# First stage of a Hymba layer: x loaded channel-major instead of token-major and transposed

## The chip, the core and the metric

One NeuronCore of a Trainium2 chip runs the whole layer in one launch. The metric is the time of one execution on the device, in microseconds (us). The engines are named as the profile names them: PE is the matrix engine (TensorE), PEld its weight loads, DVE the VectorE, ACT the ScalarE, POOL the GpSimd, SP the engine that only issues transfers. Each engine works through its own queue of instructions in order and waits on semaphores of the others; a waiting instruction holds up everything behind it on the same engine.

## What is computed

The layer takes x (1024 tokens by 1024 channels, float32) and a vector cond, from which shifts, scales and gates are made. The change touches the beginning of the first of three sublayers:

```python
def rms_norm(x, gain):
    y = xf * lax.rsqrt(jnp.mean(xf * xf, axis=-1, keepdims=True) + EPS)
    return (y * gain.astype(jnp.float32)).astype(x.dtype)

def modulate(h, shift, scale):
    return h * (1 + scale[:, None, :]) + shift[:, None, :]

def swiglu(h, w_gate, w_up, w_down):
    return (jax.nn.silu(h @ w_gate) * (h @ w_up)) @ w_down
...
    c_act = jax.nn.silu(cond)
    mod = c_act @ w_mod[l] + b_mod[l]
...
    h = modulate(rms_norm(x, ffn1_norm[l]), sh1, sc1)
    x = x + 0.5 * g1[:, None, :] * swiglu(h, ffn1_w_gate[l], ffn1_w_up[l], ffn1_w_down[l])
```

The mean of squares runs over the 1024 channels of a token. What is called x after this stage is the modulated h; the original x is loaded again much later for the residual.

## The kernel before

The products need h with channels on the 128 partitions and tokens along the free axis. There are 8 channel tiles (k = 0 to 7) and two halves of 512 tokens (h = 0, 1), so 16 tiles `x[k][h]` of 128x512. To keep float32 accuracy each operand is split in two parts of a shorter float32 format: ACT casts it to the part `hi`, DVE subtracts to get `lo`, and a product is three matmuls (`mm3`, line 330: hi·hi, hi·lo, lo·hi). For activations the split is `shifted` and `lows`, for weights it is `weight` (a cast and a subtraction of 128x1024).

The stage around the change builds four products (`part`, line 926; outputs 0 and 2 are gate columns, 1 and 3 the up columns that go with them) over 8 k-tiles and two halves: 64 parts of three matmuls, 192 matmuls in all, named `p` in the profile. When they are done PE goes on with the next group of the same sublayer, named `fa1`.

Before a `p` matmul can run on a tile, this is done:

- x is loaded token-major (`tok_load`, from a second copy of x): eight tiles `xb` of 128 tokens by 1024 channels, four for each half. With tokens on partitions the sum of squares is one instruction with an accumulator for each tile (`squares`, line 848), on DVE or ACT by choice.
- `root_of` turns the four sums of a half into four columns of 1/rms: a small DVE instruction and a power on POOL.
- `scaled` multiplies the tokens' rows by it, in pieces of some k-tiles: on ACT, a small piece on POOL.
- `turned` (line 892) transposes: four PE transposes of 128x128 for each k and h, into a PSUM tile `pt`; 16 such groups in all.
- `shifted` (line 898) on ACT reads `pt`, applies the channel's scale and shift, writes `x[k][h]`, and casts it to `hi`; `lows` on DVE makes `lo`.
- `mods_of(k)` (line 858) makes the scale and the shift of the 128 channels of k: two DVE reductions over a loaded tile `mw` of 1 MB.

`kept_busy` puts matmuls whose result nobody reads on PE (named `filler`).

The order of everything in the stage is the order of the source (`InOrder.strict` ties each engine's instructions to their order in the code); there is no planner here. Lines 935 to 1018 are that order. All loads are issued from SP in the order of the code: four tiles of x, one `mw`, two raw weight tiles, the other four tiles of x, and so on.

Of the kernel before, what the change touches and what calls it, by code (L numbers as in the profile page):

```python
# [40 lines left out]
ENDS = 2, 3, 6, 7  # L41
J = S // TAU
# [189 lines left out]
def hymba_layer(ctx: ExitStack, tc, x_d, xt_d, wm1_d, wmod_d, gu1_d, gs1_d, ds10_d, ds11_d, wl1_d, win_d, wcvb_d, wout_d, glu_d, gu2_d, gs2_d, wd2_d, ds20_d, ds21_d, ds22_d, wl2_d, cols_d, cond_d, lam_d, bc_d, out_d):  # L232
# [575 lines left out]
    tok_open = ExitStack()  # L808
    tok = tok_open.enter_context(tc.tile_pool(name="tok", bufs=1, side="right"))
# [7 lines left out]
    mw, xb = [], []  # L817
    pre = t2k("pre")[:, :KT]
    st = t2k("st")
    junks = [mov(f"junk{i}", dtype=F32)[:].rearrange("p a b -> p (a b)") for i in range(2)]  # L820

    def mod_load(n=1):
        for _ in range(n):
            k = len(mw)
            mw.append(pro.tile([P, 2, 1024], F32, tag="mw", name=f"mw{k}", bufs=3))
            SP.dma_start(mw[k][:], wm1_d[k])

    def tok_load(n):
        for _ in range(n):
            b = len(xb)  # L830
            if b < 4:
                xb.append(tok.tile([P, D], F32, tag=f"xb{b}", name=f"xb{b}")[:])
            else:
                xb.append(mov(f"xb{b}", dtype=F32)[:].rearrange("p a b -> p (a b)"))
            SP.dma_start(xb[b], xt_d[b])

    tok_load(4)
    mod_load()
    ws.load(2)

# [7 lines left out]
    def squares(b, engine):  # L848

        if engine is A:  # L850
            A.activation(junks[-1], xb[b], AF.Square, accum_out=st[:, b : b + 1])
        else:
            other = junks[0]
            V.tensor_tensor_reduce(
                out=other, in0=xb[b], in1=xb[b], scale=1.0, scalar=0.0, op0=ALU.mult, op1=ALU.add, accum_out=st[:, b : b + 1]
            )
# [11 lines left out]
    root = [None, None]  # L868
# [5 lines left out]
    def scaled(h, lo, hi, engine=A):  # L874

        for b in range(4):
            part, by = xb[4 * h + b][:, lo * P : hi * P], root[h][:, b : b + 1]
            if engine is A:
                A.activation(part, part, AF.Identity, scale=by)
            else:  # L880
                engine.tensor_scalar(out=part, in0=part, scalar1=by, scalar2=None, op0=ALU.mult)

    turns = {}
    filler = ps("filler")

    def kept_busy(n, lhsT, rhs):

        for _ in range(n):
            T.matmul(filler[:], lhsT=lhsT, rhs=rhs, start=True, stop=True)


    def turned(h, k):

        turns[h, k] = sm([P, HALF], f"pt{k}_{h}")
        for b in range(4):
            T.transpose(turns[h, k][:, b * P : (b + 1) * P], xb[4 * h + b][:, k * P : (k + 1) * P], ident[:])

    def shifted(h, k):

        hi, lo = act1[h][k] = parts(f"h1{k}_{h}")  # L900
        A.activation(x[k][h], turns.pop((h, k))[:], AF.Identity, bias=mods[:, 0, k : k + 1], scale=scl[:, 0, k : k + 1])
        A.copy(hi, x[k][h])

    def lows(h, k):
        hi, lo = act1[h][k]
        V.tensor_tensor(out=lo, in0=x[k][h], in1=hi.bitcast(F32), op=ALU.subtract)

    w4 = []

    def weight(home):  # L910
        ws.open(home, 1)
        w4.extend(ws.take())
# [22 lines left out]
    squares(0, V)  # L935
    squares(1, V)
    silu(0)
    silu(1)
    squares(2, A)
    squares(3, V)  # L940
    tok_load(4)
    mod_load()
    ws.load(4)
    mod_load()
    kept_busy(4, ident[:], xb[0][:, :HALF])
    root_of(0)
    scaled(0, 0, 2)
    mods_of(0)
    mod_load()
    turned(0, 0)  # L950
# [3 lines left out]
    turned(0, 1)  # L954
    part(0, 0, (0,))
    weight(ringp)
    part(0, 0, (1,))
    kept_busy(18, w4[0][:, 0, :P], act1[0][0][0])
    squares(4, A)
    squares(5, A)  # L960
    squares(6, V)
    squares(7, V)
    scaled(0, 2, 8)
    root_of(1)
    scaled(1, 0, 2)
    scaled(1, 2, 4, nc.gpsimd)
    turned(1, 0)
    kept_busy(3, w4[0][:, 0, :P], act1[0][0][0])
    mods_of(1)
    mod_load()  # L970
    weight(ringp)
    shifted(1, 0)
    shifted(0, 1)
    lows(1, 0)
    mods_of(2, (0,))
    turned(1, 1)
    part(1, 0, (0, 1, 2))
    part(0, 0, (2,))
    lows(0, 1)
    turned(0, 2)  # L980
    shifted(1, 1)
    part(0, 1, (0, 1, 2))
    lows(1, 1)
    mods_of(2, (1,))
    mod_load()
    turned(1, 2)
    shifted(0, 2)
    part(1, 1, (0, 1, 2))
    lows(0, 2)
    mods_of(3)  # L990
    mod_load()
    shifted(1, 2)
    scaled(1, 4, 8)
    lows(1, 2)
    for k in range(2, KT):
        if k + 1 < KT:
            turned(0, k + 1)
        part(0, k, (0, 1, 2))
        if k + 1 < KT:
            turned(1, k + 1)  # L1000
            shifted(0, k + 1)
            shifted(1, k + 1)
        if k + 2 < KT:
            mods_of(k + 2)
            if k + 5 < KT:
                mod_load()
        if k + 1 < KT:
            lows(0, k + 1)
            lows(1, k + 1)
        if k == 5:  # L1010
            weight(ringp)
        part(1, k, (0, 1, 2))
    for h in range(2):
        part(h, 0, (3,))
    gu_first(0)
    for k in range(1, KT):
        for h in range(2):
            part(h, k, (3,))
    InOrder.strict = False
    tok_open.close()  # L1020
# [3 lines left out]
    ws.free(3)  # L1024
    ws.free()
# [958 lines left out]
_ORDER = ["x", "xt", "wm1", "wmod", "gu1", "gs1", "ds10", "ds11", "wl1", "win", "wcvb", "wout", "glu", "gu2", "gs2", "wd2", "ds20", "ds21", "ds22", "wl2", "cols", "cond", "lam", "bc"]  # L1984
# [17 lines left out]
```

## Time and profile before

| | |
|---|---|
| median of 3 runs | 1650.75 us (1650.39 to 1652.87) |
| profiled execution | 1650.02 us, of it the span that the profile shows 1648.3 us |
| PE busy | 1631.4 us (99%) |
| DVE busy | 1142.9 us (69%) |
| ACT busy | 721.8 us (44%) |
| POOL busy | 177.7 us (11%) |

The span begins with the first instruction and all times in rows are counted from there. PE's share of busy time counts pipelined matmuls and is no measure of its speed, but a stretch without a gap on PE means that PE is what the stretch waits for. The stage of the change reaches from the start of the span to 75.44 us, where the first `fa1` matmul starts.

### The profile page before, as it was taken

To read this page: it belongs to the slowest core of one execution; us is meant where nothing else is said; L and a number is where in the kernel's file an instruction comes from. 1 tells how busy PE (TensorE), PEld (TensorE's weight loads), DVE (VectorE), ACT (ScalarE), POOL (GpSimd) and SP (SyncE) were. 2 spreads that over 40 slices of the span, in tenths; PEclk is the share of its full clock that TensorE was granted. 3 is DMA by queue.
4 is the path that set the end of the run, shared out by engine and by line. 5 is a ranking of instruction groups with operands and counts; after the bars stand their busy time and mean duration, and the time that the engine had idled before them with its cause. 6 is when DMAs were issued, how large, how long until landed. Compare 5 with 4: busy or idle time off the path is not lost.

```text
span 1648.3 us, 20569 instructions
## 1 busy us (share of the span) xinstructions
PE 1631.4 (99%) x7437; PEld 1347.6 (82%) x7437; DVE 1142.9 (69%) x1688; ACT 721.8 (44%) x1072; POOL 177.7 (11%) x219
## 2 busy tenths in 40 slices
PE   8999999999999999999999999999999999999997
PEld 5888888888888888888888888888888888888887
DVE  7984487878576758887887898755565655344576
ACT  6654333333454442463234546344444444322345
POOL 2010000000100102200000030000101100010004
PEclk9999999999999999999999999999999999999999
DMA  9466789898987775668774534477788787889732
GB/s 359 141 161 159 216 221 279 248 265 245 284 242 199 199 225 199 211 199 232 202 196 142 183 102 151 118 205 216 210 221 222 216 221 217 298 250 352 225 71 102
DMA packets 130871, 346.34 MB, mean 210 GB/s; under 512 B 16849, under 2 KB 40657, under 8 KB 129746
## 3 DMA queue, kind: packets, MB, share of 16 engines
q1 hardware_dynamic: 112338, 278.97, 48.6%
q0 software_dynamic: 18432, 66.07, 23.1%
q8 instruction: 58, 0.95, 0.2%
q14 instruction: 43, 0.35, 0.1%
HBM read 261.75 MB, written 74.84 MB: 204 GB/s over the span
## 4 chain that ended last, share of the span: by engine, by line
PE 92%; DVE 3%; ACT 1%; issue 1%; DMA 1%; POOL 1%; SPq 0%; POOLq 0%; DVEq 0%; ACTq 0%
PE wo L113 5%; PE fbd_1B L113 3%; PE fbd_0B L113 3%; PE u L113 3%; PE fad_0B L113 3%; PE fad_1B L113 3%; PE p L113 3%; PE fald L113 2%; PE fbd_1C L113 1%; PE fbd_0C L113 1%; PE gl L113 1%; PE fb0d L113 1%; PE fad_1C L113 1%; PE fad_0C L113 1%; PE fb10d L113 1%; PE fb0u L113 1%
## 5 line engine op out<-in xcount | busy, mean ns | idle before, releaser
L113 DVE TENSOR_TENSOR w<-raw,w 128x1024 fp32r<-128x1024 f32 (+1 forms) x256 | 309.4, 1209 | 235.3 <-ACT w L113 234.8
L113 ACT CAST w<-raw 128x1024 fp32r<-128x1024 f32 (+1 forms) x256 | 266.2, 1040 | 287.6 <-DMA raw<-in_ds 59.9
L175 POOL DMA_DIRECT2D raw<-in_gs x80 | 70.4, 883 | 732.4 <-DVE w L113 431.1
L113 DVE CUSTOM_DVE_ANT_0 wm<-wm,cact 128x1024 f32<-128x1024 f32 x56 | 74.4, 1347 | 2.9 <-DMA wm<-in_wmod 2.9
L175 POOL DMA_DIRECT2D raw<-in_ds x36 | 31.5, 877 | 310.2 <-DVE w L113 207.4
L113 PE MATMUL p<-h,w 128*128 128x512 f32 x192 | 49.0, 404 | 2.0 <-ACT h L113 1.5
L113 PE MATMUL wo<-oa,w 128*128 128x512 f32 x192 | 45.1, 392 | 0.0
L113 PE MATMUL wo<-ob,w 128*128 128x512 f32 x192 | 44.9, 392 | 0.0
L113 PE MATMUL u<-h,w 128*128 128x512 f32 x192 | 44.4, 391 | 0.0
L113 PEld LDWEIGHTS p<-h,w 128*128 128x128 f32 x192 | 35.3, 190 | 10.4 <-ACT h L113 2.0
L113 PEld LDWEIGHTS u<-h,w 128*128 128x128 f32 x192 | 35.8, 188 | 7.6 <-issue 0.3
L113 PEld LDWEIGHTS wo<-ob,w 128*128 128x128 f32 x192 | 35.7, 188 | 7.4
L113 PEld LDWEIGHTS wo<-oa,w 128*128 128x128 f32 x192 | 35.7, 188 | 7.2
L175 POOL DMA_DIRECT2D raw<-in_wcvb x12 | 10.6, 880 | 145.9 <-DVE w L113 69.1
L113 PE MATMUL fb0u<-h,w 128*128 128x512 f32 x96 | 23.8, 391 | 0.0
L113 PE MATMUL fb0g<-h,w 128*128 128x512 f32 x96 | 23.2, 389 | 0.0
L113 PE MATMUL fald<-fa9lA,w 128*128 128x512 f32 x96 | 22.8, 392 | 0.0
L113 PE MATMUL gl<-yg,w 128*128 128x512 f32 x96 | 22.7, 392 | 0.0
L113 PE MATMUL fald<-fa0lA,w 128*128 128x512 f32 x96 | 22.4, 389 | 0.0
L113 PE MATMUL fald<-fa10lA,w 128*128 128x512 f32 x96 | 22.4, 389 | 0.0
L113 PEld LDWEIGHTS fb0g<-h,w 128*128 128x128 f32 x96 | 18.0, 188 | 3.8
L113 PEld LDWEIGHTS fald<-fa0lA,w 128*128 128x128 f32 x96 | 18.0, 188 | 3.7
(1656 smaller groups left out, 4039.1 us busy)
## 6 DMA issues: line engine op xcount, KB each, us to landing
raw<-in_gs SPq DMA_DIRECT2D x80, 512.0 KB, 4.7
raw<-in_gs POOLq DMA_DIRECT2D x80, 512.0 KB, 6.5
wm<-in_wmod SPq DMA_DIRECT2D x56, 512.0 KB, 6.5
raw<-in_ds SPq DMA_DIRECT2D x32, 512.0 KB, 4.1
raw<-in_ds POOLq DMA_DIRECT2D x32, 512.0 KB, 7.3
mw<-in_wm SPq DMA_DIRECT2D x8, 1024.0 KB, 7.7
raw<-in_wcvb SPq DMA_DIRECT2D x12, 512.0 KB, 5.5
raw<-in_wcvb POOLq DMA_DIRECT2D x12, 512.0 KB, 6.8
```

Of the source, the lines that this page charges most:

```text
L113: r = getattr(self.engine, name)(*args, **kw)
L175: self.G.dma_start(out=r, in_=src, accum_op=ALU.add)
```

## The change

x is loaded channel-major, straight into the tiles `x[k][h]` (`load_x`, four transfers of 128x1024 for each half). Four things follow:

- With channels on partitions the sum over channels runs across partitions. ACT squares a pair of k-tiles (128x1024), DVE adds the two (128x512), and PE multiplies each 128x128 piece with a column of ones: four matmuls with one output column for each pair, 16 for each half, accumulated in a PSUM tile `pst`.
- 1/rms is wanted along the free axis on all partitions: four matmuls of the columns, widened, with the identity spread it into a PSUM tile `pbc`. `root_kept` copies that to SBUF (`pbk`) for all k but the first.
- The transposes are gone. `scaled` is now one DVE instruction for each tile (x times the channel's scale times the spread root, in place), and `shifted` adds the shift on ACT, in place, and casts.
- Loads are in another order, and four `mw` tiles in place of three are held. Output 3 is no longer left to the end for all k: all four outputs run for k = 2 to 5, and only for k = 6 and 7 outputs 2 and 3 come last (`LATE`). `gu_first(0)` and the freeing of weight slots move with that. The filler matmuls are 2 and 8, before 4, 18 and 3.

The core of the diff:

```diff
-    tok_load(4)
+    load_x((0,))
     mod_load()
     ws.load(2)
+    mod_load()
+    load_x((1,))
+    ws.load(3)
+    mod_load()
+    ws.load(4)
+    mod_load(MW - 3)
...
+    def squares(h, j):
+
+        sq = mov(f"psq{j}_{h}", dtype=F32)
+        A.activation(sq[:], xt[j][h][:], AF.Square)
+        V.tensor_tensor(out=sq[:, 0, :], in0=sq[:, 0, :], in1=sq[:, 1, :], op=ALU.add)
+        for i in range(4):
+            T.matmul(
+                st[h][:, i : i + 1], lhsT=sq[:, 0, i * P : (i + 1) * P], rhs=one[:], start=j == i == 0, stop=j == 3, skip_group_check=True
+            )
...
     def root_of(h):
-        root[h] = t2k(f"py{h}")[:, :4]
-        roots(st[:, 4 * h : 4 * h + 4], 4, D, f"p{h}", root[h])
+        y = pro.tile([P, 4], F32, name=f"py{h}")
+        roots(st[h][:, :4], 4, D, f"p{h}", y[:], True)
+        across[h] = sm([P, HALF], f"pbc{h}")
+        for i in range(4):
+            T.matmul(across[h][:, i * P : (i + 1) * P], lhsT=y[:, i : i + 1].to_broadcast([P, P]), rhs=ident[:], start=True, stop=True)
+
+    def root_kept(h):
+        t = pro.tile([P, HALF], F32, name=f"pbk{h}")
+        A.copy(t[:], across[h][:])
+        across[h] = t
...
-    def turned(h, k):
-
-        turns[h, k] = sm([P, HALF], f"pt{k}_{h}")
-        for b in range(4):
-            T.transpose(turns[h, k][:, b * P : (b + 1) * P], xb[4 * h + b][:, k * P : (k + 1) * P], ident[:])
+    def scaled(h, k):
+
+        V.scalar_tensor_tensor(out=x[k][h], in0=x[k][h], scalar=scl[:, 0, k : k + 1], in1=across[h][:], op0=ALU.mult, op1=ALU.mult)
...
     def shifted(h, k):
         hi, lo = act1[h][k] = parts(f"h1{k}_{h}")
-        A.activation(x[k][h], turns.pop((h, k))[:], AF.Identity, bias=mods[:, 0, k : k + 1], scale=scl[:, 0, k : k + 1])
+        A.activation(x[k][h], x[k][h], AF.Identity, bias=mods[:, 0, k : k + 1])
         A.copy(hi, x[k][h])
...
+    kept_busy(2, ident[:], x[0][0])
+    for j in range(4):
+        squares(0, j)
     root_of(0)
...
+    kept_busy(8, w4[0][:, 0, :P], act1[0][0][0])
     mods_of(1)
     mod_load()
+    squares(1, 0)
+    modulated1(0, 1)
+    squares(1, 1)
+    part(0, 1, (0, 1))
+    squares(1, 2)
+    squares(1, 3)
+    root_of(1)
     weight(ringp)
+    part(0, 0, (2,))
+    part(0, 1, (2,))
+    scaled(1, 0)
     shifted(1, 0)
...
+    for k in range(2, KT):
+        scaled(0, k)
+        shifted(0, k)
+        scaled(1, k)
+        if k + 1 < KT:
+            mods_of(k + 1, (0,))
+        lows(0, k)
+        part(0, k, range(4 if k < LATE else 2))
+        shifted(1, k)
+        if k + 1 < KT:
+            mods_of(k + 1, (1,))
+        if len(mw) < KT:
+            mod_load()
+        lows(1, k)
+        part(1, k, range(4 if k < LATE else 2))
+    gu_first(0)
+    ws.free(2)
+    for k in range(LATE, KT):
+        for h in range(2):
+            part(h, k, (2, 3))
```

`modulated1(h, k)` is `scaled`, `shifted` and `lows` in a row. In the orders below a name like `p1_0` is output 1 of half 0, `h11_0` the split tile of k = 1 and half 0, `psq1_1` the squares of the second pair of half 1.

PE from the first products of half 0 to the first of half 1, before:

```order
L113 MATMUL p0_0_205<-h10_0_196,w0_193 128x512 x3
L113 MATMUL p1_0_214<-h10_0_196,w1_209 128x512 x3
L113 MATMUL filler_147<-h10_0_196,w0_193 128x512 x18
L113 MATMUL pt0_1_256<-ident_84,xb4_156 128x128
L113 MATMUL pt0_1_256<-ident_84,xb5_158 128x128
L113 MATMUL pt0_1_256<-ident_84,xb6_160 128x128
L113 MATMUL pt0_1_256<-ident_84,xb7_162 128x128
L113 MATMUL filler_147<-h10_0_196,w0_193 128x512 x3
```

The same place on PE now:

```order
L114 MATMUL p0_0_207<-h10_0_203,w0_200 128x512 x3
L114 MATMUL p1_0_218<-h10_0_203,w1_213 128x512 x3
L114 MATMUL filler_153<-h10_0_203,w0_200 128x512 x8
L114 MATMUL pst1_123<-one_89,psq0_1_234 128x1 x4
L114 MATMUL pst1_123<-one_89,psq1_1_246 128x1 x4
L114 MATMUL p0_0_207<-h11_0_242,w0_200 128x512 x3
L114 MATMUL p1_0_218<-h11_0_242,w1_213 128x512 x3
L114 MATMUL pst1_123<-one_89,psq2_1_259 128x1 x4
L114 MATMUL pst1_123<-one_89,psq3_1_266 128x1 x4
L114 MATMUL pbc1_277<-ident_84,py1_273 128x128 x4
L114 MATMUL p2_0_288<-h10_0_203,w2_282 128x512 x3
L114 MATMUL p2_0_288<-h11_0_242,w2_282 128x512 x3
```

Between the products of half 0 and those of half 1 stood eight transposes and the fillers; now it is the sums of squares of half 1, the spread of its root, and four parts of half 0 that came later before.

ACT between the first cast of half 0 and the root of half 1, before:

```order
L113 CAST h10_0_196<-x0_0_106 128x512
L113 CAST w1_209<-raw1_140 128x1024
L113 ACTIVATE junk1_127,st_125<-xb4_156 128x1024
L113 ACTIVATE junk1_127,st_125<-xb5_158 128x1024
L113 ACTIVATE xb0_128<-xb0_128,py0_176 128x768
L113 ACTIVATE xb1_130<-xb1_130,py0_176 128x768
L113 ACTIVATE xb2_132<-xb2_132,py0_176 128x768
L113 ACTIVATE xb3_134<-xb3_134,py0_176 128x768
L113 ACTIVATE xb4_156<-xb4_156,py1_244 128x256
```

The same place on ACT now:

```order
L114 CAST h10_0_203<-x0_0_106 128x512
L114 COPY pbk0_211<-pbc0_192 128x512
L114 CAST w1_213<-raw1_132 128x1024
L114 ACTIVATE psq0_1_234<-x0_1_110 128x1024
L114 ACTIVATE x0_0_106<-x0_0_106,mods_95 128x512
L114 CAST h11_0_242<-x0_0_106 128x512
L114 ACTIVATE psq1_1_246<-x1_1_111 128x1024
L114 ACTIVATE psq2_1_259<-x2_1_112 128x1024
L114 ACTIVATE psq3_1_266<-x3_1_113 128x1024
L114 ACTIVATE p1nv_274<-pst1_123,eps_91 128x4
L114 CAST w2_282<-raw2_140 128x1024
```

Before, half 1 had two squares on ACT (and two on DVE) with nothing of half 0 in front of them but finished work; now the second, third and fourth square of half 1 stand behind the shift and the cast of k = 1 of half 0.

DVE at that place now, from the multiply of the first tile of half 0 on:

```order
L114 SCALAR_TENSOR_TENSOR x0_0_106<-x0_0_106,scl_96,pbc0_192 128x512
L114 TENSOR_TENSOR w0_200<-raw0_130,w0_200 128x1024
L114 TENSOR_TENSOR h10_0_203<-x0_0_106,h10_0_203 128x512
L114 TENSOR_TENSOR w1_213<-raw1_132,w1_213 128x1024
L114 ISA mw1_134,scl_96<-mw1_134,cact_102,pre_121,cols_83 128x1024
L114 ISA scl_96 128x1
L114 ISA mw1_134,mods_95<-mw1_134,cact_102,cols_83 128x1024
L114 ISA mods_95 128x1
L114 TENSOR_TENSOR psq0_1_234<-psq0_1_234 128x512
L114 SCALAR_TENSOR_TENSOR x0_0_106<-x0_0_106,scl_96,pbk0_211 128x512
L114 TENSOR_TENSOR h11_0_242<-x0_0_106,h11_0_242 128x512
L114 TENSOR_TENSOR psq1_1_246<-psq1_1_246 128x512
```

The multiplies are new on DVE, and the one for k = 1 of half 0 stands behind the two reductions of `mods_of(1)`.

## Rows read from the trace of the kernel before

**Rows 1.** Windows: busy time of each engine and granted clock (PEclk) by stretch.

```profile
core 0: us, PE busy (x) PEld busy (x) DVE busy (x) ACT busy (x) POOL busy (x), PEclk, DMA share, GB/s
...
0.00:27.60 27.60, 21.50 (x57) 11.36 (x57) 17.45 (x30) 18.72 (x30) 7.52 (x13) 0.94 0.93 362
27.60:75.44 47.84, 47.84 (x233) 39.56 (x234) 44.86 (x70) 33.54 (x52) 3.56 (x4) 1.00 0.56 181
75.44:150.00 74.56, 74.56 (x330) 61.74 (x329) 50.55 (x116) 38.99 (x62) 7.34 (x40) 1.00 0.63 159
```

**Rows 2.** Chain of waits up to 120 us: start, us, what.

```profile
27.60 2.81 PE p L113 x11
30.41 0.44 PE pt L113 x4
...
58.57 17.04 PE p L113 x75
```

**Rows 3.** Timeline, first 45 us: start, us, engine, line, operation, idle and releaser.

```profile
8.31 1.06 ACT L113 ACTIVATE junk<-xb 128x1024 f32<-128x1024 f32 x1 [1.56 <-DMA xb<-in_xt]
...
9.62 0.34 PEld L113 LDWEIGHTS filler<-xb,ident 128*128 128x128 f32 x1 [0.52 <-issue]
9.65 1.23 DVE L113 CUSTOM_DVE_ANT_0 junk<-xb 128x1024 f32<-128x1024 f32 x1 [1.62 <-DMA xb<-in_xt]
10.47 0.32 PEld L113 LDWEIGHTS filler<-xb,ident 128*128 128x128 f32 x1 [0.52 <-issue]
...
11.04 0.19 PEld L113 LDWEIGHTS filler<-xb,ident 128*128 128x128 f32 x1 [0.24 <-issue]
11.33 1.02 POOL L399 TENSOR_TENSOR py<-p0nv,power 128x4 f32<-128x4 f32 x1 [10.03 <-DVE p0nv L113]
...
12.09 1.34 DVE L113 CUSTOM_DVE_ANT_0 mw<-mw,cact,pre 128x1024 f32<-128x1024 f32 x1 [0.91 <-DMA mw<-in_wm]
...
13.36 1.28 DVE L113 CUSTOM_DVE_ANT_0 mw<-mw,cact,cols 128x1024 f32<-128x1024 f32 x1
...
13.99 1.03 ACT L113 CAST w<-raw 128x1024 fp32r<-128x1024 f32 x1
...
15.06 1.23 DVE L113 TENSOR_TENSOR w<-raw,w 128x1024 fp32r<-128x1024 f32 x1 [0.41 <-ACT w L113]
...
22.42 1.34 DVE L113 CUSTOM_DVE_ANT_0 mw<-mw,cact,pre 128x1024 f32<-128x1024 f32 x1 [0.79 <-DMA mw<-in_wm]
```

**Rows 4.** Timeline of PE alone, first 30 us.

```profile
6.04 6.01 PE L113 MATMUL filler<-xb,ident 128*128 128x512 f32 x8
...
17.13 2.28 PE L113 MATMUL p<-h,w 128*128 128x512 f32 x5 [0.22 <-DVE h L113]
19.20 5.12 PE L113 MATMUL filler<-h,w 128*128 128x512 f32 x18
```

**Rows 5.** Windows of one us, columns as in the first group.

```profile
15.00:16.00 1.00, 0.00 (x0) 0.00 (x0) 0.94 (x1) 0.97 (x3) 0.00 (x0) 1.00 1.03 422
...
18.00:19.00 1.00, 1.00 (x4) 0.53 (x3) 0.87 (x2) 0.97 (x3) 0.00 (x0) 0.50 1.04 426
...
21.00:22.00 1.00, 1.00 (x6) 0.83 (x5) 0.50 (x3) 1.00 (x3) 0.29 (x1) 1.00 0.96 397
```

**Rows 6.** Timeline of the second sublayer's norm, which has the new operations already.

```profile
673.70 0.69 DVE L113 TENSOR_TENSOR n2aq<-n2aq,n2aq 128x512 f32<-128x512 f32 x1
...
675.65 1.08 PEld L113 LDWEIGHTS n2ast<-one,n2aq 128*128 128x128 f32 x8
...
677.02 0.26 ACT L113 ACTIVATE n2anv<-n2ast,eps 128x4 f32<-128x4 f32 x1
...
679.33 1.16 PE L113 MATMUL n2abc<-ident,n2any 128*128 128x128 f32 x8 [0.31 <-POOL n2any L399]
...
680.53 2.06 DVE L113 SCALAR_TENSOR_TENSOR h2t<-x,scl,n2abc 128x512 f32<-128x512 f32 x3 [2.15 <-PE n2abc L113]
681.37 0.73 ACT L113 ACTIVATE h2t<-h2t,mods 128x512 f32<-128x512 f32 x1 [4.09 <-DVE h2t L113]
...
682.13 0.62 ACT L113 CAST h<-h2t 128x512 fp32r<-128x512 f32 x1
```

More of the change, by code (lines that the diff above doesn't have):

```diff
@@ L41 @@
 ENDS = 2, 3, 6, 7
+MW, LATE = 4, 6
 J = S // TAU
@@ L816, in hymba_layer @@
     SP.dma_start(cols[:], cols_d)
-    mw, xb = [], []
+    mw = []
     pre = t2k("pre")[:, :KT]
-    st = t2k("st")
-    junks = [mov(f"junk{i}", dtype=F32)[:].rearrange("p a b -> p (a b)") for i in range(2)]
+    st = [ps(f"pst{h}") for h in range(2)]
     def mod_load(n=1):
@@ L824, in mod_load @@
             k = len(mw)
-            mw.append(pro.tile([P, 2, 1024], F32, tag="mw", name=f"mw{k}", bufs=3))
+            mw.append(pro.tile([P, 2, 1024], F32, tag="mw", name=f"mw{k}", bufs=MW))
             SP.dma_start(mw[k][:], wm1_d[k])
[L828 to L835, printed above, removed]
-    tok_load(4)
+    load_x((0,))
     mod_load()
     ws.load(2)
+    mod_load()
[4 more added lines that the diff above has]
+    mod_load(MW - 3)
     b1 = cols[:, C_BMOD + SC1 * KT : C_BMOD + (SC1 + 1) * KT]
@@ L846, in hymba_layer @@
         T.matmul(cps[i][:], lhsT=ones, rhs=crow[:, i * 512 : (i + 1) * 512], start=True, stop=True)
[L848 to L855, printed above, removed]
+    def squares(h, j):
[5 more added lines that the diff above has]
+                st[h][:, i : i + 1], lhsT=sq[:, 0, i * P : (i + 1) * P], rhs=one[:], start=j == i == 0, stop=j == 3, skip_group_check=True
             )
@@ L866, in mods_of @@
             )
-    root = [None, None]
+    across = [None, None]
     def root_of(h):
-        root[h] = t2k(f"py{h}")[:, :4]
-        roots(st[:, 4 * h : 4 * h + 4], 4, D, f"p{h}", root[h])
-    def scaled(h, lo, hi, engine=A):
-        for b in range(4):
[L877 to L883, printed above, removed]
+        y = pro.tile([P, 4], F32, name=f"py{h}")
[7 more added lines that the diff above has]
+        across[h] = t
     filler = ps("filler")
@@ L889, in kept_busy @@
             T.matmul(filler[:], lhsT=lhsT, rhs=rhs, start=True, stop=True)
-    def turned(h, k):
-        turns[h, k] = sm([P, HALF], f"pt{k}_{h}")
-        for b in range(4):
-            T.transpose(turns[h, k][:, b * P : (b + 1) * P], xb[4 * h + b][:, k * P : (k + 1) * P], ident[:])
+    def scaled(h, k):
+        V.scalar_tensor_tensor(out=x[k][h], in0=x[k][h], scalar=scl[:, 0, k : k + 1], in1=across[h][:], op0=ALU.mult, op1=ALU.mult)
     def shifted(h, k):
         hi, lo = act1[h][k] = parts(f"h1{k}_{h}")
-        A.activation(x[k][h], turns.pop((h, k))[:], AF.Identity, bias=mods[:, 0, k : k + 1], scale=scl[:, 0, k : k + 1])
+        A.activation(x[k][h], x[k][h], AF.Identity, bias=mods[:, 0, k : k + 1])
         A.copy(hi, x[k][h])
@@ L906, in lows, with modulated1 @@
         V.tensor_tensor(out=lo, in0=x[k][h], in1=hi.bitcast(F32), op=ALU.subtract)
+    def modulated1(h, k):
+        scaled(h, k)
+        shifted(h, k)
+        lows(h, k)
     w4 = []
@@ L933, in silu @@
         A.activation(cact[:, i * 512 : (i + 1) * 512], cps[i][:], AF.Silu)
-    squares(0, V)
-    squares(1, V)
     silu(0)
     silu(1)
[L939 to L945, printed above, removed]
+    kept_busy(2, ident[:], x[0][0])
+    for j in range(4):
+        squares(0, j)
     root_of(0)
-    scaled(0, 0, 2)
     mods_of(0)
-    mod_load()
-    turned(0, 0)
+    scaled(0, 0)
     weight(ringp)
@@ L953, in hymba_layer @@
     lows(0, 0)
-    turned(0, 1)
     part(0, 0, (0,))
+    root_kept(0)
     weight(ringp)
     part(0, 0, (1,))
[L958 to L968, printed above, removed]
+    kept_busy(8, w4[0][:, 0, :P], act1[0][0][0])
     mods_of(1)
     mod_load()
+    squares(1, 0)
@@ L971, in hymba_layer @@
+    modulated1(0, 1)
[4 more added lines that the diff above has]
+    root_of(1)
     weight(ringp)
+    part(0, 0, (2,))
+    part(0, 1, (2,))
+    scaled(1, 0)
     shifted(1, 0)
-    shifted(0, 1)
+    mods_of(2, (0,))
     lows(1, 0)
-    mods_of(2, (0,))
-    turned(1, 1)
     part(1, 0, (0, 1, 2))
-    part(0, 0, (2,))
-    lows(0, 1)
-    turned(0, 2)
+    root_kept(1)
+    scaled(1, 1)
     shifted(1, 1)
-    part(0, 1, (0, 1, 2))
-    lows(1, 1)
     mods_of(2, (1,))
@@ L985, in hymba_layer @@
     mod_load()
-    turned(1, 2)
-    shifted(0, 2)
+    lows(1, 1)
     part(1, 1, (0, 1, 2))
[L989 to L1016, printed above, removed]
+    weight(ringp)
+    for k in range(2):
         for h in range(2):
             part(h, k, (3,))
+    for k in range(2, KT):
[13 more added lines that the diff above has]
+        part(1, k, range(4 if k < LATE else 2))
@@ L1019, in hymba_layer @@
+    gu_first(0)
[3 more added lines that the diff above has]
+            part(h, k, (2, 3))
     InOrder.strict = False
-    tok_open.close()
     kept.update({g: Kept(f"kept{g}", g not in LAST[0], False, g in LAST[0]) for g in range(1, NGRP)})
     gu_first(1)
-    ws.free(3)
-    ws.free()
+    ws.free(2)
     pro_open.close()
@@ L1981, in _arrays @@
     return {k: np.ascontiguousarray(v) for k, v in a.items()}
[L1984 removed]
+_ORDER = ["x", "wm1", "wmod", "gu1", "gs1", "ds10", "ds11", "wl1", "win", "wcvb", "wout", "glu", "gu2", "gs2", "wd2", "ds20", "ds21", "ds22", "wl2", "cols", "cond", "lam", "bc"]
 def kernel(**inputs):
```

5 lines of the change are left out of this document (1 added, 4 removed).

## The prediction

> **What bounds the kernel now.** I read the windows first, for where PE stands still; then the chain of waits, for what the first stage waits for; then the timeline of its first 45 us; and last the one place where the kernel already does what the change brings in, the norm of the second sublayer. The reader is to see in the windows that PE has a gap only at the start: 21.5 of the first 27.6 us are busy, and from there to 150 us everything is [rows 1]. So the time is set by when PE's unbroken stream begins and by how much PE has to do in it, and the stage ends at 75.44. The stream begins at 27.60 and consists of `p` matmuls, 75 in 17.04 us or 0.227 each, and groups of four transposes, 0.44 each [rows 2]. Any us by which the stage ends later is lost in full, since PE waits for nothing afterwards that a later start would shorten.
>
> **What goes from PE's stream.** Of the 16 groups of transposes four are done before 27.60, so 12 are on the path: 12 x 0.44 = 5.3 us. The fillers cost nothing themselves: they fill time in which PE has nothing else. The squares and the scaling by rows go from ACT and DVE in the stretch before 27.60, and with them what they allowed: half 1 of x needed only its own tiles and free engines.
>
> **What comes before the stream, half 0.** Loads up to `mw0` have the same order and sizes, so the fourth x tile is used at 9.65 as before [rows 3]. Its square on ACT takes 1.06 [rows 3], the add on DVE 0.69 [rows 6]: 11.4. PE is not free for the sums before 9.6: each float32 filler is two passes, the eight start at 6.04 [rows 4] and are 0.85 apart (the loads at 9.62 and 10.47 [rows 3]), and of four fillers two stay. A group of sums for one pair of k-tiles is eight weight loads with one output column; the same form took 1.08 in the second norm, and ACT read the result 1.37 after the group's start (675.65 to 677.02) [rows 6]. From 9.6 on four groups are due one after the other, and the fourth starts at 12.8, or at about 13.5 because PE's clock is still low at first (below). Then come, by the second norm's rows: 1.37 to ACT's small instruction; 0.26 for it and 0.1 to POOL, 1.02 for the power on POOL [rows 3], 0.05 to the spread, together 1.43; 1.20 from spread to multiply (679.33 to 680.53); 0.84 to the shift; 0.76 to the cast; 0.67 to the first matmul [rows 6]. The multiply of half 0 starts at 13.5 + 1.37 + 1.43 + 1.20 = 17.5, its cast ends at 19.7.
>
> **Half 1 stands in a queue.** This is the step that decides. On ACT its second to fourth square stand behind the shift of k = 1 of half 0; that waits for a multiply which on DVE stands behind the subtraction for `w1` and the two reductions of `mods_of(1)`. Counted from 19.7: ACT's copy of the spread (bounded by the casts, I take 0.5) and the cast of `w1`, 1.03, end at 21.2; the subtraction, 1.23 [rows 3], at 22.4; the reductions, 12.09 to 14.64 or 2.5 [rows 3], at 24.9; the first pair's add and the multiply, 0.6 and 0.7, at 26.2; shift and cast at 27.5. An engine takes its next independent instruction about 0.1 before the last is done, so three squares of 1.06 end at 30.4, and the last add at 31.2. The first of these three adds is done at 29.3, and from there PE has a group of sums, six matmuls of `part(0, 1, (0, 1))`, and two groups. With the clock high that is 1.08 + 1.36 + 1.08, and the last group starts at 32.8. The root follows as above, 34.2 for ACT's instruction, 36.8 for the multiply (the subtraction for `w2`, new in front of it on DVE, is done at 36.6 and just hidden), 39.1 for the first matmul of half 1. The second k-tile of half 1 waits for the copy of its spread on ACT and for a multiply, shift and cast behind it, and starts some 2.75 later, 41.8. By then 9 of 64 parts are done, and 55 x 3 x 0.227 = 37.5 plus one wait of 0.5 for `lo` ends the stage at 79.8. That is 4.4 later than 75.44. The balance says the same: the first matmul of half 1 comes 12.3 later than the one before (26.8, a us before the stream), four parts more are done by then (2.7), and 5.3 of transposes are saved.
>
> **The clock.** The second thing that decides. With the granted clock at 0.50 the filler and `p` matmuls took about twice as long: five in 2.28 against 0.227 each [rows 2, 4], 4 in a window against 6 [rows 5]. This is the level of 1.2 GHz in place of 2.4. The row says 1.00 before 17 us, but the fillers' loads stand 0.85 apart until 10.47 and then 0.57 [rows 3], so PE was at the lower level there too, and rose after eight us of dense work. It fell after the stretch around 15 us with no matmul in it and rose at 21 in the middle of 18 dense fillers [rows 4, 5]. Now there are 8 fillers at 22.6, and behind them PE is idle or loads weights for one column until the stream. I take the lower level from 29 to about 47. What a group of sums costs there no row shows: below, 1.08 if its pace is set elsewhere; above, 2.16 if all of it is PE's clock. The weight loads show 0.34 at the lower level against 0.19 at the higher [rows 3], so I take the upper end. Then the last group of half 1 starts at 29.3 + 2.16 + 6 x 0.43 + 2.16 = 36.2, ACT reads at 38.6, the spread takes 2.2 and the multiply is at 42.2; first matmul 44.5, second k-tile 47.2, end 85.2: 9.8 later. A rise somewhere within the chain gives some of it back, so I take 9.
>
> **What I cost at nothing.** The other order of loads: the last x tile of half 1 lands where `mw1` landed before, 22.4 [rows 3], and its square does not run before 27.5; if that cover went, each us would count. In the loop from k = 2 DVE has two multiplies, two subtractions and two reductions for each k, 4 x 0.61 + 2.47 = 4.9, and PE 8 parts or 5.4; but for k = 6 PE has only 4 parts before it wants k = 7, so over the five rounds to that tile it is 24.5 on DVE against 4 x 5.44 + 2.72 = 24.5 on PE, and only DVE's start, half an us ahead, hides it. The multiply from SBUF is bounded by 0.69 and 0.74 [rows 6]. In the next group the weights are made later than before: the last part with `w0` ends 9 parts (6.1) before the stage's end, a cast and a subtraction later, 3.4 before the end, `w7`'s accumulating transfer can be issued, and 48 matmuls (10.9) after the end `w7` is read: 14.3 for that transfer, a cast and a subtraction of 2.3 together. That stays hidden.
>
> **The rivals.**
> - The clock is back early and high in half 1's chain: 4.4 later, 1655.2. For it: the 8 fillers and the matmuls before them are a dense stretch of some four us, as the one that ended at 21 was. Against: 3 us without a matmul follow.
> - The clock stays low through half 0 as well, since the sums replace the fillers that ran when it rose before: the fourth group starts at 16.1 in place of 13.5, the rest of that chain has 1.0 twice more, the multiply of half 0 is at 22.1, and all later steps by 4.6: 14.4 later, 1665.2. The Trainium skill, page "TensorE: Matmul & The Clock Gate", section "HAM oscillation — how this bites in real kernels", holds that gaps on PE put the slow clock back and that it is paid again at each burst of work; by that rule this rival or the forecast is the case, and the rows around 15 and 18 us agree.
> - Not slower: the squares of half 1 do not wait in ACT's queue. With the last x tile at 22.4 they would end at 23.5, the add at 24.2, 7.0 earlier than 31.2, and with a high clock the stage would end at 72.8, 2.6 earlier: 1648.1. It decides from a first matmul of half 1 at 34.7 or earlier. Against it stands ACT's order, in which the shift of k = 1 comes before them.
> - DVE becomes the bound in the loop: there is half an us of lead in five rounds, so 0.7 more on DVE for each k, by waits of its own or slower reductions, makes PE stand for about 3 on top of the forecast: 1662.8.
> - The change does as it says: the transposes were on the path, not hidden. There is no rival in that.
>
> **How the numbers follow.** The profiled execution took 1650.02, 1.7 more than its span and 0.7 less than the median, so differences are added to the median of 1650.75. Chances: the forecast, 9 later or 1659.8, 0.46; high clock 0.22; low throughout 0.19; DVE 0.07; not slower 0.06. The range that leaves 2 in 10 out reaches from just below the high clock's case to the low one's, 1654.5 to 1665. A change of 0.2% (3.3 us) is about what a measurement tells here. Of the high clock's case, which stands one us above that, a quarter falls within; with the lower edge of the forecast and the upper one of the last rival that makes 0.10 for the same, 0.05 for faster and 0.85 for slower.
>
> **What would show it.** In the new profile: the chain of waits runs through the squares on ACT, the sums on PE and the power on POOL twice; ACT is idle for about four us before the shift of k = 1 of half 0; the first matmul of half 1 stands between 39 and 45, and the stream after it has no gap and no transposes; a group of sums takes near 2 us where the granted clock is 0.50. It is wrong if half 1's squares run before 25 us, if the stream begins before 35, or if PE waits in the loop or in the first groups of `fa1`.

## The result, and the profile after

The changed kernel takes 1661.74 us (median of 4 runs, 1660.95 to 1664.4), the kernel before 1651.65 beside it: a ratio of 1.0061, with a 95% interval from 1.0049 to 1.0073. That is 10.1 us slower; 9 were forecast. (Against the 1650.75 to which the forecast was added it is 11.0.) Its profiled execution took 1662.2 us with a span of 1660.4, 12.1 more than the span of before.

The windows of the changed kernel, cut where the first matmul of half 1 has its weights loaded (45.44; the matmul itself starts at 45.53) and where the first `fa1` matmul starts (PE busy, granted clock, DMA share, GB/s), answer to [rows 1]:

```profile
0.00:45.44 45.44, 35.71 (x114) 0.85 0.82 312
45.44:87.12 41.68, 41.03 (x175) 1.00 0.27 83
87.12:150.00 62.88, 62.72 (x277) 1.00 0.71 179
```

The stage ends at 87.12 in place of 75.44, 11.7 later. From there the distance stays: the second group `fa2` starts 12.2 later than before, the third sublayer's norm 12.2, and the span ends 12.1 later. In this execution, everything that the change did to the time it did before 87.12, but for half a us in `fa1`.

Timeline of the changed kernel, half 0 (start, us, engine, line, operation, idle before it and what ended that); it answers to [rows 3, 4]:

```profile
9.53 6.83 PE L114 MATMUL pst<-one,psq 128*128 128x1 f32 x32
...
16.39 0.26 ACT L114 ACTIVATE p0nv<-pst,eps 128x4 f32<-128x4 f32 x1 [5.89 <-PE pst L114]
...
16.81 1.03 POOL L400 TENSOR_TENSOR py<-p0nv,power 128x4 f32<-128x4 f32 x1 [15.50 <-ACT p0nv L114]
...
17.89 2.08 PE L114 MATMUL pbc<-ident,py 128*128 128x128 f32 x8 [1.53 <-POOL py L400]
20.00 0.75 DVE L114 SCALAR_TENSOR_TENSOR x<-x,scl,pbc 128x512 f32<-128x512 f32 x1 [5.39 <-PE pbc L114]
...
21.60 0.62 ACT L114 CAST h<-x 128x512 fp32r<-128x512 f32 x1
```

The four groups of sums start at 9.5, as forecast, but take 1.7 each to the last; the spread takes 2.08 where the second norm's took 1.16 [rows 6]. By these durations PE was at the lower level for the whole of half 0: two groups of sums take 3.41 further down, where the granted clock reads 0.50. (The clock's row reads 1.00 here; the last section says why that does not count.)

The same view for half 1, without most rows of PE's weight loads:

```profile
23.55 1.06 ACT L114 ACTIVATE psq<-x 128x1024 f32<-128x1024 f32 x1
...
24.82 1.34 DVE L114 CUSTOM_DVE_ANT_0 mw<-mw,cact,pre 128x1024 f32<-128x1024 f32 x1
...
27.90 0.74 DVE L114 SCALAR_TENSOR_TENSOR x<-x,scl,pbk 128x512 f32<-128x512 f32 x1
...
28.68 0.72 ACT L114 ACTIVATE x<-x,mods 128x512 f32<-128x512 f32 x1 [4.08 <-DVE x L114]
...
29.96 2.94 ACT L114 ACTIVATE psq<-x 128x1024 f32<-128x1024 f32 x3
...
32.93 0.69 DVE L114 TENSOR_TENSOR psq<-psq 128x512 f32<-128x512 f32 x1 [0.26 <-ACT psq L114]
...
33.51 2.91 PE L114 MATMUL p<-h,w 128*128 128x512 f32 x6
...
36.21 3.41 PE L114 MATMUL pst<-one,psq 128*128 128x1 f32 x16
39.72 0.26 ACT L114 ACTIVATE p1nv<-pst,eps 128x4 f32<-128x4 f32 x1 [6.81 <-PE pst L114]
...
41.12 2.07 PE L114 MATMUL pbc<-ident,py 128*128 128x128 f32 x8 [1.50 <-POOL py L400]
...
43.23 0.75 DVE L114 SCALAR_TENSOR_TENSOR x<-x,scl,pbc 128x512 f32<-128x512 f32 x1 [1.06 <-PE pbc L114]
```

This is the forecast's queue, row by row. ACT did half 1's first square at 23.6, then stood idle for 4.08 before the shift of k = 1 of half 0, which waited for DVE, and only behind it came the three other squares. Then PE's chain runs at half speed, as the windows of one us show:

```profile
28.00:29.00 1.00, 1.00 (x7) 1.00 1.00 422
...
32.00:33.00 1.00, 1.00 (x6) 0.50 1.00 418
44.00:45.00 1.00, 1.00 (x4) 0.50 0.93 168
...
46.00:47.00 1.00, 0.83 (x4) 1.00 1.01 410
```

Behind the fillers, at 28.73, a group of sums takes 0.95, so the clock is high there; then PE has nothing to do for 2.1 us, the clock is at the lower level by 32, and it is back at 46, when the stream begins. From 48.97 on PE has almost no gap, and no transposes (timeline of PE; it answers to [rows 2]):

```profile
48.97 31.27 PE L114 MATMUL p<-h,w 128*128 128x512 f32 x135 [0.22 <-DVE h L114]
80.40 6.88 PE L114 MATMUL p<-h,w 128*128 128x512 f32 x29 [0.16 <-DVE h L114]
87.12 1.07 PE L114 MATMUL fa1gB<-h,w 128*128 128x512 f32 x4
```

Its 164 matmuls from 48.97 to 87.12 take 38.15, 0.9 more than at 0.227 each. Most of that lies near 78 and 80 us, at k = 7, where PE's weight loads wait for DVE twice (timeline of the weight loads from 78 to 81 us):

```profile
78.59 1.23 PEld L114 LDWEIGHTS p<-h,w 128*128 128x128 f32 x6 [0.47 <-DVE h L114]
80.40 0.76 PEld L114 LDWEIGHTS p<-h,w 128*128 128x128 f32 x4 [0.58 <-DVE h L114]
```

### The profile page after: what moved, and what is told of

Its sections match the earlier page's. It is cut to its first block, busy times and chain, and to the rows that moved or that the text cites. A ratio compares the mean times of both kernels' runs of the same rounds, so it can differ in the third digit from the quotient of the medians.

```text
span 1660.4 us, 20551 instructions
## 1 busy us (share of the span) xinstructions
PE 1639.6 (99%) x7436; PEld 1356.8 (82%) x7436; DVE 1152.4 (69%) x1700; ACT 716.8 (43%) x1062; POOL 171.4 (10%) x215
## 4 chain that ended last, share of the span: by engine, by line
PE 89%; issue 5%; DVE 4%; POOL 1%; DMA 1%; ACT 0%; POOLq 0%; DVEq 0%; ACTq 0%; SPq 0%
PE wo L114 5%; PE fald L114 3%; PE fbd_1B L114 3%; PE fbd_0B L114 3%; PE u L114 3%; PE fad_1B L114 3%; PE fad_0B L114 3%; PE fbd_1C L114 1%; PE fbd_0C L114 1%; PE gl L114 1%; PE fad_1C L114 1%; PE fad_0C L114 1%; PE fb0d L114 1%; PE fb10d L114 1%; PE fb0u L114 1%
## 5 line engine op out<-in xcount | busy, mean ns | idle before, releaser
L114 ACT ACTIVATE x<-x,mods 128x512 f32<-128x512 f32 x16 | 11.6, 723 | 25.1 <-DVE x L114 25.1
```

Of the source, the lines that this page charges most:

```text
L114: r = getattr(self.engine, name)(*args, **kw)
```

## The experiments

Every ratio is to the kernel before, run beside them. The theory: half 1 waits in the queues of ACT and DVE, and PE's short steps run at the lower clock; the rivals are named with each run.

**1. Half 1's squares ahead.**

```diff
+    for j in range(4):
+        squares(1, j)
     mods_of(1)
     mod_load()
-    squares(1, 0)
     modulated1(0, 1)
-    squares(1, 1)
     part(0, 1, (0, 1))
-    squares(1, 2)
-    squares(1, 3)
     root_of(1)
```

> The edit: half 1's four squares and its sums are issued ahead of the reductions for k = 1 and of the multiply and shift of k = 1 of half 0; nothing else moves. Queue theory (half 1 is late because its squares stand behind that shift on ACT): the squares run from 23.6 to 27.6, the last add ends near 28.2 in place of 33.6, the four groups of sums follow the fillers on PE from 28.9 and end between 33.2 (1.08 each) and 35.8 (1.7 each) in place of 39.6; the first matmul of half 1 comes 4 to 6.4 earlier than 45.4, and the time falls by as much, to 1655.3 to 1657.7. Rival (the low clock on PE's chain is all of it, the squares' place does not decide): the time falls by less than 1.

Measured: 1656.86 us, ratio 1.0036 (1.0023 to 1.0048), 4.9 less than the changed kernel. Its timeline:

```profile
9.98 3.80 PE L114 MATMUL pst<-one,psq 128*128 128x1 f32 x32
...
21.92 3.90 ACT L114 ACTIVATE psq<-x 128x1024 f32<-128x1024 f32 x4
...
27.17 3.90 PE L114 MATMUL pst<-one,psq 128*128 128x1 f32 x32
...
34.16 1.91 PE L114 MATMUL pbc<-ident,py 128*128 128x128 f32 x8
```

The squares run in one piece and the stage ends at 80.01, 7.1 earlier. Of this 1.6 is not the edit's: here half 0's sums, the same instructions as in the changed kernel, took 3.80 in place of 6.83, and its multiply came at 18.38 in place of 20.00. The other 5.5 is the queue: the last add ends at 26.54 in place of 33.62, 7.1 earlier, and from there to the first matmul of half 1 it is 11.8 in both kernels. Of the 7.1 the group `fa1` gives 0.8 back, where PE waits for DVE's adds, and the span comes out 5.6 shorter.

**2. Fillers in half 1's chain.** Four behind its first group of sums, four behind its last.

```diff
     squares(1, 0)
+    kept_busy(4, w4[0][:, 0, :P], act1[0][0][0])
     modulated1(0, 1)
...
     squares(1, 3)
+    kept_busy(4, w4[0][:, 0, :P], act1[0][0][0])
     root_of(1)
```

> The edit: two times four filler matmuls, behind the first group of sums of half 1 and behind the last; nothing else. Clock theory (from 31.8 to 45.5 the granted clock is 0.50 because PE had nothing dense before, and it doubles what PE does in half 1's chain): the clock stays at 1.00, the six p matmuls take 1.4 in place of 2.9, the last two groups of sums 2.1 in place of 3.4, the spread 1.2 in place of 2.1; less 0.5 for the fillers' own delay, the first matmul of half 1 comes 3 to 4 earlier than 45.4 and the time falls to 1657.7 to 1658.7. Rival (PE's clock in this chain does not matter, ACT's and DVE's order does): no gain, and up to 2 later by the fillers themselves.

Measured: 1662.35, ratio 1.0063 (1.0049 to 1.0077): nothing gained. The windows of this run (columns as above) say why:

```profile
30.00:31.00 1.00, 0.99 (x4) 1.00 1.05 442
...
33.00:34.00 1.00, 1.00 (x5) 0.50 1.12 463
...
42.00:43.00 1.00, 1.00 (x7) 0.79 0.65 57
43.00:44.00 1.00, 1.00 (x6) 1.00 0.75 78
```

The clock fell all the same, to 0.50 by 33, and the p matmuls and the last sums took 2.91 and 3.41 as before. It came back at 42, three us earlier than without the fillers, when nearly all of the chain was done. So the edit doesn't test what a high clock would give; it shows that eight fillers don't buy it. What would keep the clock up through these sums stays open.

**3. One group of sums for a half.** DVE adds the four pairs, PE has four matmuls in place of sixteen.

```diff
         V.tensor_tensor(out=sq[:, 0, :], in0=sq[:, 0, :], in1=sq[:, 1, :], op=ALU.add)
-        for i in range(4):
+        if j:
+            V.tensor_tensor(out=sq[:, 0, :], in0=sq[:, 0, :], in1=sums[h], op=ALU.add)
+        sums[h] = sq[:, 0, :]
+        for i in range(4 if j == 3 else 0):
```

> The edit: DVE adds the four pairs of k-tiles into one tile (three more adds of 0.69 for each half), and PE has one group of four sums for each half in place of four. If the sums on PE at the low clock (6.83 for half 0, 1.86 and 3.41 for half 1) are on the path: half 0's last add ends at 11.9, its one group at 13.6, and its multiply comes 2.7 earlier than 20.0; half 1's last add comes at about 31.6 and its one group ends near 33.3 in place of 39.6; the time falls by 5 to 6.5, to 1655.2 to 1656.7. Rival (only the squares' place on ACT and DVE counts, PE's sums lie beside it): the three adds come on top, no gain or 1.4 later.

Measured: 1658.83, ratio 1.0046 (1.0034 to 1.0059), 2.9 less than the changed kernel, about half of what was expected. In its timeline

```profile
12.80 1.84 PE L114 MATMUL pst<-one,psq 128*128 128x1 f32 x8 [3.07 <-DVE psq L114]
...
33.55 1.84 PE L114 MATMUL pst<-one,psq 128*128 128x1 f32 x8 [1.93 <-DVE psq L114]
```

half 0's root is 1.7 earlier (14.68 against 16.39), half 1's 4.2 (35.48 against 39.72), and the stage ends 4.2 earlier (0.8 of it is lost again between 499 and 621 us in this profile). PE's sums at the lower level are on the path, but DVE's additions take their place: two for each pair, 1.3, against ACT's pace of 0.95, which the expectation had overlooked.

**4. Four fillers at the start,** as the kernel before had.

```diff
-    kept_busy(2, ident[:], x[0][0])
+    kept_busy(4, ident[:], x[0][0])
```

> The edit: four fillers in place of two at the start, as many as the kernel before had. Clock theory (the fillers that went are why PE's clock did not rise at 10.8 in half 0's chain): the clock rises at about 10.8, the fillers end at 11.9, the four groups of sums take 1.08 each and end at 16.2 as now, the spread takes 1.2 in place of 2.1 and the first six matmuls less, so the time falls by about 1, to 1660.7. Rival (two fillers more do not raise it): the sums start 3.4 later at the same pace, and the time rises by 3.4, to 1665.

Measured: 1663.29, ratio 1.0076 (1.0063 to 1.0088). The mechanism is as expected: behind the longer fillers the sums run at the higher level, 3.63 in all, and half 0's root comes at 15.07, 1.3 earlier than in the changed kernel's profile; the stage ends 1.3 earlier, at 85.82. The time is no better. With two fillers the sums can run at the higher level too (experiments 1, 5 and 7), and then start 1.4 to 1.8 sooner; in this profiled run `fa1` lost 0.7 more than in the changed kernel's; and 1.7 went in the third sublayer's norm, where its clock was 0.83 for a stretch of ten us and the kernel before had 1.00. That last loss, 1.6 each time, with such a stretch at the lower level, is also in the profiles of experiments 5, 6, 7, 8 and 10, and in none of the others: a single profile's span can hold it or not. Why the median is 1.5 up is not settled.

**5. The spread ahead of six p matmuls.** On the first experiment, `root_of(1)` stands before `part(0, 1, (0, 1))`.

> The edit: half 1's squares ahead, as in the first run, and in PE's order also half 1's spread ahead of the six p matmuls of k = 1 of half 0. In the first run the power on POOL was done at 32.7 and the spread began at 34.2, behind these six, which took 3.2 at the low clock. If that wait is on the path: the time falls by about 1.5 against the first run's 1656.9, to 1655.4. Rival (the six only change places with the wait, since they must run before the stream anyway): under 0.5.

Measured: 1657.03, ratio 1.0033 (1.0021 to 1.0046): the rival. The spread did begin at 32.1, right behind POOL, and the stage ended at 78.16, 1.85 earlier than in the first experiment (0.6 of it because half 0's multiply came earlier), yet the time is the same. In the profiled run 1.5 are lost between 499 and 621 us, which the first experiment's profile doesn't lose there, and more in the third norm; what in other runs takes it back stays open.

**6. The edits together.** The order of the fifth, sums in two groups for a half, four fillers at the start, two and four around half 1's sums.

```diff
-    kept_busy(8, w4[0][:, 0, :P], act1[0][0][0])
+    kept_busy(2, w4[0][:, 0, :P], act1[0][0][0])
+    for j in range(4):
+        squares(1, j)
+    root_of(1, 4)
     mods_of(1)
...
-        for i in range(4):
+        if j % 2:
+            V.tensor_tensor(out=sq[:, 0, :], in0=sq[:, 0, :], in1=sums[h], op=ALU.add)
+        sums[h] = sq[:, 0, :]
+        for i in range(4 if j % 2 else 0):
```

> The edits together: half 1's squares and spread ahead; DVE adds the pairs two by two, so that PE has two groups of sums for a half in place of four; four fillers in place of two at the start, two in place of eight behind the first p matmuls, four behind half 1's last sums. If the queue and PE's groups of sums are what the change lost: half 0's sums end at about 13.8 (16.4), its multiply comes at 17.5 (20.0), half 1's sums end near 28 (39.6) and its first matmul is at 33.6 to 34.4 (45.4), some 11 earlier; the time comes to 1650.5 to 1652.5, no longer to be told from the kernel before. Rival (something else in the stage, DVE in the loop or the weights behind it, ends it as late): above 1655.

Measured: 1654.92 (9 runs), ratio 1.0020 (1.0010 to 1.0030): two thirds of the loss are gone, but 1650.5 to 1652.5 was expected, and that was missed. The roots come at 13.29 and 27.18 in place of 16.39 and 39.72, and the stage ends at 76.39, one us behind the kernel before. The waits of PE behind the stage (engine, line, what it waited for, us in total, times, longest):

```profile
PE fa1gB L114 <- DVE fa1gc L114: 1.0, 1, 1.0
PE fa1uB L114 <- DVE fa1uc L114: 0.3, 1, 0.3
```

From `fa1` to `fa2` this kernel takes 39.97, the kernel before 38.09, the changed one 38.62. DVE's adds for `fa1` stand there behind small instructions for tables of a later sublayer. These start late because DVE reaches them late and because their load, `lam`, is issued at 100.8 behind two loads of weights; DVE waited 1.6 for it. In this profile, whose execution took 1656.03, another 1.4 is lost between 499 and 621 us and 1.6 in the third norm; what causes these two is open.

**7. Twelve groups of transposes put back** into the changed kernel's stream, on x, with a result that nobody reads.

```diff
     part(1, 1, (0, 1, 2))
+    for k in range(2, KT):
+        for h in range(2):
+            turn = sm([P, HALF], f"turn{k}_{h}")
+            for b in range(4):
+                T.transpose(turn[:, b * P : (b + 1) * P], x[0][0][:, b * P : (b + 1) * P], ident[:])
```

> The edit: twelve groups of four transposes are put back into PE's stream of the changed kernel, behind the second k-tile of half 1, on a tile of x and with a result that nobody reads. If the transposes were on the path: 12 x 0.44 = 5.3 later, 1667.0. Rival (the loads or DVE set the pace of the stream, the transposes lay beside them): under 1 later.

Measured: 1667.8, ratio 1.0096 (1.0082 to 1.0110), 5.7 more than experiment 8 beside it. In PE's timeline they are one row:

```profile
48.51 5.40 PE L114 MATMUL turn<-ident,x 128*128 128x128 f32 x48
```

So the transposes were on the path. They take 5.4 on PE; at the end of the stage 4.45 of it is left (half 1's multiply comes 2.42 earlier here than in experiment 8, the stage's end 2.03 later), since behind them PE no longer waits for DVE near 80 us.

**8. The loads in the order of before.**

```diff
-    mod_load()
     load_x((1,))
-    ws.load(3)
     mod_load()
     ws.load(4)
-    mod_load(MW - 3)
+    mod_load(MW - 2)
```

> The edit: the loads in the order of the kernel before, all of half 1 of x ahead of mw1, and the third and fourth block of weights ahead of mw2; nothing else. Costed at nothing: the order of the loads does not matter, since half 1's squares wait in ACT's queue and the reductions for k = 1 in DVE's: within 0.5 of 1661.7. Rival (mw1 now lands too late for the reductions for k = 1, at 24.8): later by what they wait, one to two us.

Measured: 1662.15, ratio 1.0063 (1.0050 to 1.0076), and the stage ends at 87.12 to the hundredth. The order of the loads costs nothing.

**9. Two waits of the sixth taken away.** Half 1's multiply and shift ahead of the third block of weights, `lam` loaded at the start.

```diff
     part(0, 1, (0, 1))
+    scaled(1, 0)
+    shifted(1, 0)
     weight(ringp)
     part(0, 0, (2,))
     part(0, 1, (2,))
-    scaled(1, 0)
-    shifted(1, 0)
```

> On the version with the edits together: half 1's multiply and shift for k = 0 stand ahead of the third block's cast and subtraction (there the multiply started at 32.5, 1.2 behind the end of the spread, since DVE had the subtraction in front of it), and the table lam is loaded with the first loads in place of 100.8, behind two loads of weights in SP's queue (DVE waited 1.6 for it, and its adds for fa1, on which PE waited 1.3, stood behind). If both waits are on the path, the stage ends 1.1 earlier and the next group loses 1 less: 1652.5 to 1653.2. Rival (the stream and the group are then bound by what comes next on DVE): within 0.5 of 1654.9.

Measured: 1657.05, ratio 1.0037 (1.0023 to 1.0050), 2.1 slower than the sixth. The load did what was expected: from `fa1` to `fa2` 38.76. The other edit turned one wait into a longer one, in PE's timeline:

```profile
35.05 0.74 PE L114 MATMUL p<-h,w 128*128 128x512 f32 x2 [1.80 <-ACT w L114]
36.30 1.43 PE L114 MATMUL p<-h,w 128*128 128x512 f32 x5 [0.52 <-DVE w L114]
```

The third block's cast now came behind half 1's cast on ACT, and the six matmuls with that block stand on PE ahead of half 1's. The stage ended at 79.12, 2.7 later than in the sixth. Not all of that need be the edit's: in this profile half 1's sums took 3.77, in that of the sixth 1.02 and 1.09, and half 1's root came 1.35 later, at 28.53. The two are not separated.

**10. A reduction moved from beside POOL's power.** On the sixth:

```diff
-    mods_of(0)
+    mods_of(0, (0,))
     scaled(0, 0)
+    mods_of(0, (1,))
```

> On the version with the edits together: the second reduction for k = 0 (the shift's) stands behind half 0's multiply on DVE. There the power on POOL for half 0 took 1.88 (13.71 to 15.59) while DVE was in its second reduction (13.41 to 14.69); in the changed kernel, where DVE was idle, 1.03. Theory (POOL's small operation waits for DVE's running one and ends 0.9 behind it): POOL takes 1.0, half 0's multiply comes 0.8 earlier, its shift 0.3 later, and the time stays within 0.5 of 1654.9. Rival (POOL's longer time has nothing to do with DVE): POOL still takes 1.9, and multiply and shift come as before and 1.2 later.

Measured: 1655.02, ratio 1.0021 (1.0011 to 1.0031), the same as the sixth. Its timeline has

```profile
13.69 1.03 POOL L400 TENSOR_TENSOR py<-p0nv,power 128x4 f32<-128x4 f32 x1 [12.38 <-ACT p0nv L114]
...
15.97 0.75 DVE L114 SCALAR_TENSOR_TENSOR x<-x,scl,pbc 128x512 f32<-128x512 f32 x1 [2.61 <-PE pbc L114]
16.63 1.28 DVE L114 CUSTOM_DVE_ANT_0 mw<-mw,cact,cols 128x1024 f32<-128x1024 f32 x1
```

and that of the sixth

```profile
13.41 1.28 DVE L114 CUSTOM_DVE_ANT_0 mw<-mw,cact,cols 128x1024 f32<-128x1024 f32 x1
13.71 1.88 POOL L400 TENSOR_TENSOR py<-p0nv,power 128x4 f32<-128x4 f32 x1 [12.39 <-ACT p0nv L114]
...
16.91 0.75 DVE L114 SCALAR_TENSOR_TENSOR x<-x,scl,pbc 128x512 f32<-128x512 f32 x1 [2.21 <-PE pbc L114]
```

POOL's power takes 1.03 where DVE is idle, and ends 0.9 behind DVE's reduction where that runs: a wait of the small instruction for the long one. Taking it away made the multiply 0.9 earlier and the shift, which needs the reduction, 0.25 later.

No version beat the kernel before. The sixth comes within 0.1 to 0.3% of it.

## Why the prediction was right, and where it was off

**The transposes.** Right: 12 groups on the path, forecast at 5.3, measured at 5.4 on PE, 4.45 at the end of the stage and 5.7 in time (experiment 7).

**Half 0.** This is the step that was mis-sized. The sums' start (forecast 9.6, measured 9.53) and the small steps on ACT, DVE and POOL behind them were right, but not "the fourth starts at 12.8, or at about 13.5 because PE's clock is still low at first": the clock did not rise in the middle of the sums in the profiled run. ACT read them at 16.39 in place of 14.9, from the spread's start to the multiply it took 2.11 in place of 1.20, and the multiply came at 20.00 in place of 17.5. In the profiles of experiments 1, 5 and 7, with the same instructions up to there, the sums took 3.73 to 3.80, ACT read them at 13.4 to 13.8, earlier than forecast; but then POOL's power took 1.8 to 2.0 beside DVE's reduction, the spread 2.1 at the lower level, and the multiply came at 17.8 to 18.4. That term, POOL behind DVE, was not in the forecast, which took 1.02 from the first stage of before [rows 3]; the power of the second norm, in the same trace, had taken 1.92. So half 0 came 0.3 to 2.5 later than the sum had it, by how the clock happened to stand; which of the two the executions without a profile had is not known.

**Half 1's queue.** Right in order and in size: from the end of half 0's cast to the last add 11.5 were forecast, and 11.4 measured (22.22 to 33.62). ACT's idle time, forecast at about four us, was 4.08. The first experiment shows that it is on the path: without it 4.9 of the 10.1 are gone (5.5 at the end of the stage, with half 0's start taken out).

**The clock in half 1's chain.** Right in place: forecast at the lower level from 29 to about 47, measured from 32 to 45.5. A group of sums was put at 2.16 there, the upper bound; it took 1.7 to 1.86, and the stretch from the last add to the first matmul of half 1 11.8 in place of 13.3. This made up for part of half 0. The Trainium skill's rule that gaps on PE bring the slow clock back and that each burst of work pays for it again (page "TensorE: Matmul & The Clock Gate", section "HAM oscillation — how this bites in real kernels") agrees with the windows: 0.50 at 32, behind 2.1 us without work on PE, and high again only at 46. What a run adds is that no gap was needed. In the first experiment the clock fell twice while PE did nothing but sums of one column, one behind the other: at 13.3, in half 0's (9.98 to 13.78), and at 30.4, in half 1's (27.17 to 31.07), as its windows show:

```profile
13.00:14.00 1.00, 0.78 (x6) 0.65 1.05 430
...
30.00:31.00 1.00, 1.00 (x8) 0.68 1.11 463
```

It need not fall there: in experiment 5 it reads 1.00 through all of half 1's sums (25.24 to 28.87). What a high clock in this chain would have saved was not measured, since experiment 2 did not get one.

**The end of the stage.** Forecast 85.2, measured 87.12 in the profiled run. Of the 1.9 between, 0.9 is there when half 1 starts (44.5 forecast, 45.44 measured: half 0's 2.5 later, its own chain 1.5 shorter), and 0.9 comes in the stream. The estimate rounded 9.8 down to 9 for a rise that might come early, and the median shows 10.1. That the time landed so near is in part luck: a half 0 priced too low and a group of sums priced too high offset each other.

**What was costed at nothing.** The loads: right (experiment 8). DVE in the loop: not quite nothing. The half us of lead that the forecast counted on ran out at k = 7, and most of the stream's 0.9 is PE waiting there; in experiment 7, where the transposes give DVE a lead, these waits are gone. The next group's weights: hidden, as said; but the group lost 0.5 by another way, small DVE instructions for later tables in front of its adds. That cover was not examined.

**The rivals.** A high clock in half 1's chain did not occur. The low clock through half 0 did occur in the profiled run, so the profile shows this rival's case (chance 0.19) and not the forecast's; its stage ends 11.7 later in place of the 14.4 computed, since the sums took 1.7 and not 2.16. "Not slower" had the right mechanism and the right point: in the sixth experiment, where no square waits, half 1's first matmul starts at 35.03, its break-even was put at 34.7, and the stage ends 0.95 behind before's. DVE did not become the bound, beyond the waits just named.

**The signs it named.** ACT's idle time, the stream without transposes and sums of near 2 us where the clock is 0.50 (1.7 to 1.86) came as said; half 1's first matmul, at 45.44, stands just outside 39 to 45. Two signs of being wrong came in a small form. One of half 1's four squares did run before 25, at 23.55: the queue holds only the other three, as the forecast's own order says, and the sign should have named those. And PE did wait in the loop and in `fa1`, 0.9 and 0.5.

## What to carry to other kernels

A change that takes work from the busy engine must also be followed backwards, through the order of every queue that feeds it: here 5.3 us less work on the bound engine was outweighed by a stream that began 18 us later, and half of the loss came back by issuing squares whose data were there ahead of an instruction that waits. Short dependent steps on PE, at the start of a kernel or behind a gap, are to be priced at the lower clock, with the higher as a gain and not the other way round. A reordering that lets one instruction go first makes another one late, and the next thing in that engine's queue is the price.

## What the runs showed of the hardware

- One instruction stream starts in two ways. The 32 passes of half 0's sums took 6.83 us in the profiles of the changed kernel and of experiments 2 and 8, and 3.73 to 3.80 in those of 1, 5 and 7. The Trainium skill says that the number of slow matmuls at the start varies between runs of one kernel (page "TensorE: Matmul & The Clock Gate", section "What's actually happening"); these rows agree.
- The granted clock reads 1.00 in the changed kernel's trace from the start to 31 us, also where the sums ran at 1.7 a group, which elsewhere goes with 0.50. Before its first change in a trace the number is not to be trusted; the durations are.
- POOL's 128x4 power waited for DVE's reduction over two SBUF tiles and ended 0.9 behind it (experiments 1, 5, 6; 1.03 without it, experiment 10). The Trainium skill has the rule: a DVE instruction with two SBUF inputs contends with a GpSimd instruction that reads SBUF (page "SBUF — State Buffer", section "Who interferes with whom"); it calls the port that they share an exclusive lock, in which the order of issue decides who blocks. These rows agree: in each of them POOL's power came second, and waited.
